# Input projection of a two-layer backbone with 512 moving columns instead of 256

## The chip, the cores and the metric

The kernel runs on one core of a Trainium2 chip, in one launch. The metric is the device time of that launch in microseconds. Five engines work side by side: TensorE (matmuls, PE in the profile, with its weight loads as PEld), VectorE (DVE), ScalarE (ACT), GpSimd (POOL) and SyncE (SP), which issues most DMAs.

## The reference, cut to what matters

Two layers run over 256 latent and 256 context tokens of width 1024, all fp32. Each layer normalises and modulates its input and projects it once, with a weight of 1024 x 2560, into ten column groups of 256:

```
h  = rms(x)   * (1 + sc_a)  + sh_a          # hc: the same for the context
aq, ak, av, hq, hff, hfb, hi, hg, gu, gv = split(h @ w_in[layer])
attn = window_attention(rope(rms(aq)), rope(rms(ak)), av, context keys, sink)
hg_l = rms(hgrn(silu(hq), hff, hfb, hi)) * gain * silu(hg)     # both directions
gm   = gelu(gu) * (w_s @ rms(gelu(gv)) + b_s)                  # chunks of 128
x    = x + g_a * (concat(attn, hg_l, gm) @ w_out[layer])
x    = x + g_f * channel_mixer(h')          # layer 0: SwiGLU, layer 1: top 2 of 8 experts
```

In layer 1 the context is needed only for the recurrence's states (hff, hfb, hi) and for keys and values (ak, av, together "akv"). The output is the latent stream.

## The kernel before, in words

An fp32 product is made of three matmuls of rounded operands, high x high, low x high and high x low (`mm3`, L241, which issues L244 to L246). The activations h are kept split in `hx`, one tile for each of the eight blocks k of 128 input channels. The weights stream from DRAM in tiles of 128 x 1024 (`Stream`): SP's queue loads a raw tile, ScalarE writes its high part (L125) and VectorE its low part (L126), half a tile at each `tick`. Two split pairs are held, four for a while in layer 1.

The projection is a generator (`proj`, L529). It goes through the ten column groups in the order `ORDER0` in layer 0, and `hff`, `hfb`, then `ORDER1` in layer 1 (L2032 to L2034); `akv` holds keys and values, `aq0` and `aq1` the two halves of the queries. A group (`group`, L553) works on tiles of 128 tokens, two of the context and two latent (`TTS`), or only the latent ones in layer 1 where the context isn't needed. Tokens are the loaded operand, weights the moving one, 256 columns wide. A weight tile holds four blocks k of one group, so a group has two halves kh; a step is one half for one tile of tokens, 12 matmuls, followed by one `tick` and a `yield`. Two tiles of tokens share a PSUM bank of 512 columns. After the second half of a tile of tokens, `evac_..` brings its columns out of PSUM: a copy on ScalarE for hi, akv and aq, Gelu for gu and gv in layer 1 (a copy in layer 0), and chains of Exp, Ln, Exp with VectorE between for hff, hfb, hq and hg.

There are eight banks, two named "mm", two "t" and four "u". The projection takes the least recently freed "mm" or "u" bank and leaves two "u" banks to others (`PSPARE`).

The mixer (`mixer`, L1195) advances the other work of the layer once for every yield of the projection: the recurrence `hg`, the gated mixing `gm`, key preparation and query statistics `at0`, and the attention proper `at1`. Each starts when the groups that it needs are complete (`HG_AT`, `GM_AT`, `AT0_AT`, `AT1_AT`), which is noticed when the projection yields the next group's name; a last group is never noticed there, and what waits for it starts when the projection is through. Then what is left runs, together with fillers (modulation chunks, the first half of the output projection, in layer 1 row transposes at L1377). The framework's scheduler takes the order of the program as priority and may put a ready instruction ahead of one that isn't, so emission order sets priorities, not the exact order on an engine.

After layer 1's mixer comes the expert stage: 352 MB of expert weights stream through a ring of tiles that the earlier stream leaves behind.

Of the kernel before, what the change touches and what calls it, by code (L numbers as in the profile page):

```python
# [21 lines left out]
P = 128  # L22
# [11 lines left out]
LAT = (0, 1)  # L34
CTX = (2, 3)
TTS = (2, 3, 0, 1)
# [36 lines left out]
class Stream:  # L73
# [3 lines left out]
    def __init__(self, nc, plan, mem, raw, hl):  # L77
        self.nc, self.plan, self.mem = nc, plan, mem
        self.n_dma = self.n_split = self.n_out = self.n_done = self.part = 0
        self.raw, self.hl = {}, {}  # L80
        self.raw_free, self.hl_free = deque(), deque()
        self.heir = None
        self.excess = 0
        self.grow(raw, hl)
# [112 lines left out]
class Gen:  # L197
# [326 lines left out]
        mem.put(y)  # L524


    ALL1 = ("hff", "hfb", "hi", "akv")

    def proj(self, l):  # L529

        if l == 0:
            for name in ORDER0:
                yield from self.group(l, name, TTS)
            return
        names = ("hff", "hfb")
        self.ws.grow(0, GROWP)
        ws = self.ws.need(4)
        for i, name in enumerate(names):
            yield from self.group(l, name, CTX, ws[2 * i:2 * i + 2])
        for i, name in enumerate(names):  # L540
            yield from self.group(l, name, LAT, ws[2 * i:2 * i + 2])
        self.ws.shrink(GROWP)
        for name in ORDER1:
            yield from self.group(l, name, TTS if name in ("hi", "akv") else LAT)

    @staticmethod
    def order(l):

        if l == 0:
            return ORDER0  # L550
        return ("hff", "hfb") + tuple(ORDER1)

    def group(self, l, name, tts, ws=None):  # L553

        tag = "ctx" if tts is CTX else name
        ps, bank, first = {}, {}, None
        if name not in self.st["open"]:
            self.st["open"].add(name)
            for _ in self.mem.room(4, 6 if name == "hff" else 2):
                yield tag  # L560
            self.opened(name, l)
        for tt in tts[::2]:
            while not any(len(self.banks[k]) > PSPARE[k] for k in ("mm", "u")):
                yield tag
            b = bank[tt + 1] = self.oldest("mm", "u", spare=PSPARE)
            ps[tt], ps[tt + 1] = b[:, :256], b[:, 256:]
        for kh in range(2):
            wh, wl = (x.rearrange("p (k n) -> p k n", k=4) for x in (ws[kh] if ws else self.ws.need()))
            for tt in tts:
                ts = slice(tt * P, tt * P + P)  # L570
                for k in range(4):
                    h = self.hx[4 * kh + k]
                    new = kh == 0 and k == 0
                    i = self.mm3(ps[tt], h[:, 0, ts], h[:, 1, ts], wh[:, k], wl[:, k], new and tt % 2 == 0,
                                 kh == 1 and k == 3)
                    if new:
                        if tt % 2:
                            self.after(i, first)
                        first = i
                if kh == 1:  # L580
                    while len(self.mem.free[1]) < 2:
                        yield tag
                    getattr(self, "evac_" + name[:2])(l, tt, ps[tt], name)
                    if tt in bank:
                        self.done(bank[tt])
                self.ws.tick()
                yield tag

# [224 lines left out]
    def hgrn_scores(self, tt):  # L813
# [17 lines left out]
        E[6] = yield from self.hgrn_expo(tt, 6)  # L831
        yield
        for n, lv in enumerate(order):
            if n < 3:
                E[order[n + 1]] = yield from self.hgrn_expo(tt, order[n + 1])
# [348 lines left out]
    def begin(self, l):  # L1184
# [8 lines left out]
        self.mx, self.mxt = {}, []  # L1193

    def mixer(self, l, proj, filler, masks=None):  # L1195

        mem = self.mem
        tts = TTS if l == 0 else LAT
        self.attn_tables(l)
        gm, hg = self.flagged("gm", self.gmlp(l, tts)), self.flagged("hg", self.hgrn(l))  # L1200
        unit = lambda tt, g: self.attn_tile(l, tt, g)
        if l == 0:
            at0 = self.chain(self.attn_keys(l), self.attn_qstats(tts, 0), self.weave(*[unit(tt, 0) for tt in tts], n=NAT))
            at1 = self.chain(self.attn_qstats(tts, 1), self.weave(*[unit(tt, 1) for tt in tts], n=NAT))
        else:
            at0 = self.chain(self.attn_keys(l), self.attn_qstats(tts, 0))
            at1 = self.chain(self.attn_qstats(tts, 1), self.weave(*[unit(tt, g) for tt in LAT for g in range(2)], n=NAT1))
        sides = []
        prev = None
        waits = [[set(n), g, r] for n, g, r in ((HG_AT[l], hg, R_HG[l]), (AT0_AT, at0, R_AT[l]), (GM_AT, gm, R_GM[l]),  # L1210
                                                (AT1_AT, at1, R_AT[l]))]
        seen = set()
        cs = None
        if l == 1:
            cs = self.flagged("cs", self.hgrn_ctx_states())
            waits.append([set(HG_AT[1]), cs, 2])

        def advance():
            for s, n in list(sides):
                for _ in range(n):  # L1220
                    if next(s, self) is self:
                        sides.remove((s, n))
                        break
        if masks:
            sides.append((masks, 1))
        for name in proj:
            if name != prev:
                seen.add(prev)
                for x in list(waits):
                    if x[0] <= seen and (x[1] is not at1 or waits[0][1] is at1 and at0 not in [z for z, _ in sides]):  # L1230
                        waits.remove(x)
                        sides.append((x[1], x[2]))
                if {"hff", "hfb"} <= seen and l == 1 and self.lbt is not None:
                    mem.put(self.lbt)
                    self.lbt = None
                prev = name
            advance()
        mem.put(*self.hx)
        self.run(cs, hg, gm, self.chain(at0, at1), filler)
        mem.put(self.st["kv"], *self.st["aq"], *self.st["KT"], self.rt)  # L1240
# [520 lines left out]
    def plan(self):  # L1761
        A = self.A
        f = lambda ap, w=1024: (ap.rearrange("p a b -> p (a b)"), w)
        w_in = lambda l: [f(A["w_in"][l, COLS.index(n), h]) for n in self.order(l) for h in range(2)]
        plan = w_in(0) + [f(A["w_out0"][h, d]) for h in range(2) for d in range(4)]
        for half in range(2):
            plan += [f(A["ffn_gu"][11 * half + j, z]) for j in range(11) for z in range(2)]
            for d in list(range(8)) * (1 + half):
                plan += [f(A["ffn_d"][half, d][:, f0:f1, :], (f1 - f0) * P) for f0, f1 in ((0, 6), (6, 11))]
        plan += w_in(1) + [f(A["w_out1"][dh, 2 * a + b]) for a in range(2) for dh in range(2) for b in range(2)]  # L1770
        return plan
# [69 lines left out]
    def build(self):  # L1841
        nc, tc, A = self.nc, self.tc, self.A
        with ExitStack() as ctx:
# [7 lines left out]
            ps = ctx.enter_context(tc.tile_pool(name="ps", bufs=1, space=PSUM))  # L1851
# [15 lines left out]
            w = [self.ada_load(0, n) for n in (0, 2)]  # L1867
# [13 lines left out]
            next(nm)  # L1881
            for _ in range(4):
                next(nm)
            for _ in range(4):
                next(proj)
            self.run(self.ada_chunk(0, 1, w[2]))
            self.run(self.ada_chunk(0, 3, w[3]))
            self.run(nm)
            mem.put(*self.Xt)
            masks = self.load_masks()  # L1890
            for _ in range(4):
                next(proj)

            def filler0():
# [129 lines left out]
PSPARE = dict(mm=0, u=2)  # L2024
# [4 lines left out]
NAT = 4  # L2029
NAT1 = 4  # L2030
GROW0A = 2
COLS = ("hff", "hfb", "hi", "hq", "akv", "aq0", "aq1", "hg", "gu", "gv")  # L2032
ORDER0 = ('hi', 'hq', 'hff', 'hfb', 'aq0', 'aq1', 'hg', 'gu', 'gv', 'akv')
ORDER1 = ('gu', 'gv', 'akv', 'aq0', 'aq1', 'hi', 'hq', 'hg')  # L2034
EARLY = (0, 1)
HG_AT, R_HG = (('hff', 'hfb'), ('hff', 'hfb', 'gv', 'hi', 'hq')), (1, 2)
GM_AT, R_GM = ("gu", "gv"), (1, 1)
# [36 lines left out]
def _layout(inp):  # L2074
    g = {k: np.asarray(v) for k, v in inp.items()}
    c = np.ascontiguousarray
    d = _consts()
# [7 lines left out]
    d["bcol"] = c(g["b_ada"].reshape(2, 48, P).transpose(2, 0, 1))  # L2085
    o = dict(aq0=(0, 256), aq1=(256, 512), akv=(512, 768), hq=(768, 1024), hff=(1024, 1280), hfb=(1280, 1536),
             hi=(1536, 1792), hg=(1792, 2048), gu=(2048, 2304), gv=(2304, 2560))
    cols = np.concatenate([np.arange(*o[n]) for n in COLS])
    w = g["w_in"][:, :, cols]
    d["w_in"] = c(w.reshape(2, 2, 4, P, 10, 256).transpose(0, 4, 1, 3, 2, 5))  # L2090
    w = g["w_out"]
    d["w_out0"] = c(w[0].reshape(KD, P, KD, P)[list(Gen.KORD)].reshape(2, 4, P, 4, 2, P).transpose(0, 3, 2, 4, 1, 5)
                    .reshape(2, 4, P, 8, P))
# [1 line left out]
    gu = np.stack([g["ffn_w_gate"][0], g["ffn_w_up"][0]], 0)  # L2095
# [27 lines left out]
```

## Time and profile before

| | us |
|---|---|
| median of three runs | 1830.62 (1826.94 to 1834.07) |
| the profiled execution | 1828.56 |
| its span | 1826.8 |
| projection of layer 0, first and last matmul | about 25 to 183 |
| projection of layer 1 | 717 to 820 |
| expert stage | from about 930 |

The granted TensorE clock is 1.00 in both projections, and 0.987 over the span. A line of the profile's groups names the output before the arrow and the operands behind it, moving operand first; "mm" and "u" are PSUM banks. Matmuls overlap, so the time that one costs in a stream is the distance of two starts.

### The profile page before, as it was taken

The page shows a single profiled execution, that of the slowest core. Times are in us where ns is not written, and L with a number is a line of the kernel's source. Part 1 is how long each engine was busy: PE and PEld are TensorE (multiplying, and loading weights), DVE is VectorE, ACT ScalarE, POOL GpSimd, SP SyncE. Part 2 cuts the span into 40 slices and gives each one's busy share as a digit, 9 for nine tenths or more (in the row PEclk, how much of TensorE's full clock was granted, in tenths as well). Part 3 has the DMA queues.
Part 4 walks back from the last instruction along what each step waited for, and adds up shares of the span by engine and source line. Part 5 has one row for each costly group of instructions (what it writes and reads, how often), then busy time and mean ns, then how long its engine had stood idle before and what let it go on. Part 6 is the DMA issues. An engine that isn't in the chain of part 4 may idle for free. (4 is left out here: it accounts for less than half of the span.)

```text
span 1826.8 us, 34724 instructions
## 1 busy us (share of the span) xinstructions
PE 1744.1 (95%) x14056; PEld 1077.7 (59%) x14057; DVE 774.9 (42%) x1924; ACT 536.0 (29%) x1203; POOL 33.3 (2%) x56
## 2 busy tenths in 40 slices
PE   6999999999999999999989998999989999999997
PEld 3999778988788898998843333333333333333333
DVE  4556986899664378868720011110212011120112
ACT  4654656623222356765410010100101010010100
POOL 1000000100000001000000000000000000000000
PEclk9999999999999999999989999999999999999998
DMA  9224342367763255330589999999999999999990
GB/s 347 75 84 138 136 150 70 127 243 234 233 234 123 85 158 173 96 116 13 211 326 381 401 408 407 406 406 401 397 405 406 403 403 400 402 408 402 403 391 31
DMA packets 137006, 485.64 MB, mean 266 GB/s; under 512 B 15888, under 2 KB 17040, under 8 KB 136784
## 3 DMA queue, kind: packets, MB, share of 16 engines
q1 hardware_dynamic: 136080, 480.08, 69.3%
q8 instruction: 168, 2.75, 0.6%
q0 software_dynamic: 704, 2.36, 0.4%
q14 instruction: 54, 0.44, 0.1%
HBM read 481.33 MB, written 1.05 MB: 264 GB/s over the span
## 5 line engine op out<-in xcount | busy, mean ns | idle before, releaser
L1580 PE MATMUL u<-wr,xg 128*32 128x512 f32 (+1 forms) x5376 | 525.6, 546 | 18.5 <-issue 13.4
L1580 PEld LDWEIGHTS u<-wr,xg 128*32 128x32 f32 x5376 | 174.0, 111 | 342.6 <-issue 291.5
L1580 PE MATMUL mm<-wr,mT 128*32 128x512 f32 x2352 | 260.8, 593 | 4.3 <-ACT mh L264 1.5
L125 ACT ACTIVATE hi<-raw 128x512 fp32r<-128x512 f32 (+2 forms) x296 | 160.6, 580 | 244.5 <-PE u L246 90.6
L126 DVE TENSOR_TENSOR lo<-raw,hi 128x512 fp32r<-128x512 f32 (+2 forms) x296 | 178.7, 634 | 106.6 <-ACT hi L125 105.4
L1613 DVE TENSOR_TENSOR mh<-mh,u 128x512 f32<-128x512 f32 (+1 forms) x32 | 19.8, 619 | 411.1 <-PE u L1580 256.9
L1580 PEld LDWEIGHTS mm<-wr,mT 128*32 128x32 f32 x2352 | 77.6, 110 | 175.7 <-issue 152.0
L264 ACT ACTIVATE mh<-u 128x512 f32<-128x512 f32 (+1 forms) x64 | 34.6, 540 | 414.2 <-PE u L1580 413.7
L244 PE MATMUL u<-hx,hi 128*128 128x512 f32 (+1 forms) x384 | 142.9, 372 | 0.8 <-DVE X L1288 0.8
L245 PE MATMUL u<-hx,lo 128*128 128x512 f32 (+1 forms) x384 | 142.6, 371 | 0.0
L246 PE MATMUL u<-hx,hi 128*128 128x512 f32 (+1 forms) x384 | 142.6, 371 | 0.0
L264 ACT ACTIVATE mT<-t 128x512 f32<-128x512 f32 (+1 forms) x32 | 17.4, 544 | 256.4 <-PE t L1625 255.5
L245 PE MATMUL mm<-fx,lo 128*128 128x256 f32 (+1 forms) x264 | 85.0, 322 | 5.6 <-DVE lo L126 5.5
L244 PE MATMUL mm<-hi,hx 128*128 128x256 f32 x288 | 84.9, 296 | 3.8 <-ACT hx L264 3.0
L1631 DVE COPY mT<-t 128x256 f32<-128x256 f32 (+1 forms) x32 | 12.5, 391 | 170.8 <-PE t L1630 170.8
L244 PE MATMUL mm<-fx,hi 128*128 128x256 f32 (+1 forms) x264 | 84.4, 320 | 0.6 <-ACT hi L125 0.6
L246 PE MATMUL mm<-fx,hi 128*128 128x256 f32 (+1 forms) x264 | 83.9, 318 | 0.0
L245 PE MATMUL mm<-hi,hx 128*128 128x256 f32 x288 | 82.2, 287 | 0.4 <-DVE hx L521 0.3
L246 PE MATMUL mm<-lo,hx 128*128 128x256 f32 x288 | 81.7, 285 | 0.0
L244 PEld LDWEIGHTS u<-hx,hi 128*128 128x128 f32 x384 | 72.3, 188 | 13.6 <-DVE X L1288 1.0
L245 PEld LDWEIGHTS u<-hx,lo 128*128 128x128 f32 x384 | 72.3, 188 | 12.6
L246 PEld LDWEIGHTS u<-hx,hi 128*128 128x128 f32 x384 | 72.3, 188 | 12.3
(344 smaller groups left out, 2600.4 us busy)
## 6 DMA issues: line engine op xcount, KB each, us to landing
wr<-in_moe_g SPq DMA_DIRECT2D x224, 512.0 KB, 10.1
wr<-in_moe_u SPq DMA_DIRECT2D x224, 512.0 KB, 10.1
wr<-in_moe_d SPq DMA_DIRECT2D x224, 512.0 KB, 10.1
adat<-in_w_adaT SPq DMA_DIRECT2D x56, 512.0 KB, 4.8
raw<-in_ffn_gu SPq DMA_DIRECT2D x44, 512.0 KB, 3.5
adaw<-in_w_ada SPq DMA_DIRECT2D x40, 512.0 KB, 6.3
raw<-in_w_in SPq DMA_DIRECT2D x40, 512.0 KB, 3.6
raw<-in_ffn_d SPq DMA_DIRECT2D x24, 384.0 KB, 3.6
```

Source lines behind the costliest of these rows:

```text
L125: nc.scalar.activation(h[:, s], r[:, s], AF.Copy)
L126: nc.vector.tensor_tensor(l[:, s], r[:, s], h[:, s].bitcast(F32), op=ALU.subtract)
L244: i = mm(ps, lh, rh, start=start, stop=False, skip_group_check=True)
L245: mm(ps, ll, rh, start=False, stop=False, skip_group_check=True)
L246: self.final = mm(ps, lh, rl, start=False, stop=stop, skip_group_check=True)
L264: i = self.nc.scalar.activation(out, in_, func, **kw)
L1580: self.nc.tensor.matmul(bank[c:c + 32, :n], lhsT, rhs, start=start, stop=stop, tile_position=(0, c), skip_group_check=True)
L1613: nc.vector.tensor_tensor(h[:, 0, :n], h[:, 0, :n], U[:, :n], op=ALU.mult)
L1631: nc.vector.tensor_copy(hT[:, :m, :, 64:], pt[:, :m * 64].rearrange("p (j a s) -> p j a s", j=m, a=2))
```

## The change

Column groups go in pairs, five in each layer (`PAIRS`), with 512 moving columns: one matmul covers both groups. A tile of tokens has a whole bank, so a pair holds four banks (two in layer 1 where only latent or only context tokens run). A weight tile holds two blocks k of a pair, so a pair is worked in four parts; a step is two blocks for one tile of tokens, 6 matmuls. The bank of a tile of tokens is taken at its step of the first part and given back after its step of the last, where both groups are evacuated one after the other. The name that the mixer sees is that of the pair, and both names count as complete when the next pair begins. In layer 0 eight steps instead of four are emitted at each of the two places ahead of the mixer.

```diff
+    def group(self, l, names, tts, ws=None):
+        tag = "ctx" if tts is CTX else "+".join(names)
+        bank = {}
...
+        for i in range(4):
+            wh, wl = (x.rearrange("p (k n) -> p k n", k=2) for x in (ws[i] if ws else self.ws.need()))
             for tt in tts:
                 ts = slice(tt * P, tt * P + P)
...
+                if i == 0:
+                    while not any(len(self.banks[k]) > PSPARE[k] for k in ("mm", "u")):
                         yield tag
+                    bank[tt] = self.oldest("mm", "u", spare=PSPARE)
+                for k in range(2):
+                    h = self.hx[2 * i + k]
+                    self.mm3(bank[tt], h[:, 0, ts], h[:, 1, ts], wh[:, k], wl[:, k], i == 0 and k == 0,
+                             i == 3 and k == 1)
+                if i == 3:
+                    for z, name in enumerate(names):
+                        while len(self.mem.free[1]) < 2:
+                            yield tag
+                        getattr(self, "evac_" + name[:2])(l, tt, bank[tt][:, 256 * z:256 * z + 256], name)
+                    self.done(bank[tt])
                 self.ws.tick()
                 yield tag
...
-                seen.add(prev)
+                seen.update((prev or "").split("+"))
...
-            for _ in range(4):
+            for _ in range(8):
                 next(proj)
...
-ORDER0 = ('hi', 'hq', 'hff', 'hfb', 'aq0', 'aq1', 'hg', 'gu', 'gv', 'akv')
-ORDER1 = ('gu', 'gv', 'akv', 'aq0', 'aq1', 'hi', 'hq', 'hg')
+PAIRS = ((("hi", "hq"), ("hff", "hfb"), ("aq0", "aq1"), ("hg", "gu"), ("gv", "akv")),
+         (("hff", "hfb"), ("gu", "gv"), ("akv", "hi"), ("aq0", "aq1"), ("hq", "hg")))
```

## Rows read from the trace of the kernel before

**Rows 1.** The page, part 1: engines' busy us, share of the span, instructions.

```profile
PE 1744.1 (95%) x14056; PEld 1077.7 (59%) x14057; DVE 774.9 (42%) x1924; ACT 536.0 (29%) x1203; POOL 33.3 (2%) x56
```

**Rows 2.** Windows by stage; the first line names the columns.

```profile
core 0: us, PE busy (x) PEld busy (x) DVE busy (x) ACT busy (x) POOL busy (x), PEclk, DMA share, GB/s
...
90.00:188.00 98.00, 97.03 (x839) 92.08 (x838) 60.91 (x201) 50.45 (x110) 2.41 (x6) 1.00 0.36 123
188.00:260.00 72.00, 68.88 (x548) 52.88 (x546) 63.38 (x262) 42.45 (x123) 0.56 (x2) 1.00 0.40 142
...
750.00:820.00 70.00, 69.40 (x569) 67.38 (x569) 49.08 (x151) 46.13 (x115) 1.23 (x4) 1.00 0.39 129
820.00:890.00 70.00, 69.29 (x542) 61.95 (x540) 60.47 (x202) 37.89 (x88) 0.56 (x2) 1.00 0.15 52
```

**Rows 3.** Waits of PE, 20 to 260: us in total, times, longest.

```profile
PE mm L244 <- ACT hx L264: 3.0, 3, 2.7
PE mm L1084 <- ACT pp L264: 1.7, 1, 1.7
```

**Rows 4.** Windows in the expert stage, columns as in rows 2.

```profile
930.00:940.00 10.00, 10.00 (x96) 3.20 (x95) 0.08 (x1) 0.81 (x1) 0.00 (x0) 1.00 0.31 107
...
1000.00:1100.00 100.00, 96.06 (x944) 36.48 (x940) 12.07 (x19) 11.30 (x24) 0.00 (x0) 1.00 1.02 404
```

**Rows 5.** Windows of PE's work on `hx`, the projections: busy (count), clock, DMA.

```profile
20.00:188.00 168.00, 128.54 (x960) 0.98 0.41 145
715.00:825.00 110.00, 86.85 (x672) 1.00 0.35 116
```

**Rows 6.** Timeline of PE in layer 1's projection: start, us, engine, line, operation.

```profile
761.77 0.28 PE L244 MATMUL u<-hi,hx 128*128 128x256 f32 x1
...
764.53 0.28 PE L246 MATMUL u<-lo,hx 128*128 128x256 f32 x1
```

**Rows 7.** Timeline of PE in the feed-forward layer.

```profile
399.75 0.39 PE L245 MATMUL u<-hx,lo 128*128 128x512 f32 x1
...
411.99 0.39 PE L245 MATMUL u<-hx,lo 128*128 128x512 f32 x1
```

**Rows 8.** Timeline of PE in layer 1's output projection, tokens loaded, weights moving.

```profile
907.47 0.39 PE L246 MATMUL u<-lo,mx 128*128 128x512 f32 x1
...
910.01 0.39 PE L245 MATMUL u<-hi,mx 128*128 128x512 f32 x1
```

**Rows 9.** Timeline of ACT: one evacuation of hff, then two half splits.

```profile
71.67 0.38 ACT L264 ACTIVATE ge<-u 128x256 f32<-128x256 f32 x1 [0.41 <-PE u L246]
72.42 0.51 ACT L264 ACTIVATE gg<-ge,ones 128x256 f32<-128x256 f32 x1 [0.36 <-DVE ge L645]
72.96 0.42 ACT L264 ACTIVATE hk<-gg 128x256 f32<-128x256 f32 x1
73.28 0.40 ACT L264 ACTIVATE hg<-gg 128x256 fp32r<-128x256 f32 x1
...
82.19 1.15 ACT L125 ACTIVATE hi<-raw 128x512 fp32r<-128x512 f32 x2 [2.61 <-PE mm L245]
```

**Rows 10.** Windows of DVE's work on `uv`, then on `gsq`, layer 0.

```profile
150.00:188.00 38.00, 4.64 (x12) 1.00 0.54 183
...
150.00:188.00 38.00, 1.57 (x4) 1.00 0.54 183
```

**Rows 11.** Windows of DVE's work on `kk`, `kdup`, `aq`, `qt`, in that order.

```profile
765.00:820.00 55.00, 6.62 (x30) 1.00 0.35 116
...
765.00:820.00 55.00, 1.90 (x8) 1.00 0.35 116
...
765.00:820.00 55.00, 9.13 (x32) 1.00 0.35 116
...
765.00:820.00 55.00, 1.67 (x4) 1.00 0.35 116
```

**Rows 12.** Timeline of PE: layer 1's first and last projection matmul, row transposes, first scores.

```profile
717.00 0.37 PE L244 MATMUL u<-hi,hx 128*128 128x256 f32 x1
...
819.73 0.28 PE L246 MATMUL mm<-lo,hx 128*128 128x256 f32 x1
...
828.55 1.95 PE L1377 MATMUL t<-ident,mods 128*128 128x128 f32 x16
...
830.25 0.47 PE L1084 MATMUL mm<-KT,qt 128*128 128x512 f32 x1
```

More of the change, by code (lines that the diff above doesn't have):

```diff
@@ L524, in norm_mod @@
         mem.put(y)
-    ALL1 = ("hff", "hfb", "hi", "akv")
     def proj(self, l):
         if l == 0:
-            for name in ORDER0:
-                yield from self.group(l, name, TTS)
+            for names in PAIRS[0]:
+                yield from self.group(l, names, TTS)
             return
-        names = ("hff", "hfb")
         self.ws.grow(0, GROWP)
         ws = self.ws.need(4)
[L538 to L541, printed above, removed]
+        for tts in (CTX, LAT):
+            yield from self.group(l, PAIRS[1][0], tts, ws)
@@ L542, in proj @@
         self.ws.shrink(GROWP)
[L543 to L568, printed above, removed]
+        for names in PAIRS[1][1:]:
+            yield from self.group(l, names, TTS if "hi" in names else LAT)
@@ new lines, in group @@
+    def group(self, l, names, tts, ws=None):
+        tag = "ctx" if tts is CTX else "+".join(names)
+        bank = {}
+        for name in names:
+            if name not in self.st["open"]:
+                self.st["open"].add(name)
+                for _ in self.mem.room(4, 6 if name == "hff" else 2):
+                    yield tag
+                self.opened(name, l)
+        for i in range(4):
+            wh, wl = (x.rearrange("p (k n) -> p k n", k=2) for x in (ws[i] if ws else self.ws.need()))
@@ L569, in group @@
             for tt in tts:
                 ts = slice(tt * P, tt * P + P)
[L571 to L579, printed above, removed]
@@ L580, in group @@
-                if kh == 1:
-                    while len(self.mem.free[1]) < 2:
-                        yield tag
-                    getattr(self, "evac_" + name[:2])(l, tt, ps[tt], name)
-                    if tt in bank:
-                        self.done(bank[tt])
+                if i == 0:
+                    while not any(len(self.banks[k]) > PSPARE[k] for k in ("mm", "u")):
+                        yield tag
+                    bank[tt] = self.oldest("mm", "u", spare=PSPARE)
[3 more added lines that the diff above has]
+                             i == 3 and k == 1)
@@ L586, in group @@
+                if i == 3:
+                    for z, name in enumerate(names):
+                        while len(self.mem.free[1]) < 2:
+                            yield tag
+                        getattr(self, "evac_" + name[:2])(l, tt, bank[tt][:, 256 * z:256 * z + 256], name)
+                    self.done(bank[tt])
                 self.ws.tick()
@@ L1763, in plan @@
         f = lambda ap, w=1024: (ap.rearrange("p a b -> p (a b)"), w)
-        w_in = lambda l: [f(A["w_in"][l, COLS.index(n), h]) for n in self.order(l) for h in range(2)]
+        w_in = lambda l: [f(A["w_in"][l, n, h]) for n in range(5) for h in range(4)]
         plan = w_in(0) + [f(A["w_out0"][h, d]) for h in range(2) for d in range(4)]
@@ L1890, in build @@
             masks = self.load_masks()
-            for _ in range(4):
+            for _ in range(8):
                 next(proj)
@@ L2031 @@
 GROW0A = 2
-COLS = ("hff", "hfb", "hi", "hq", "akv", "aq0", "aq1", "hg", "gu", "gv")
-ORDER0 = ('hi', 'hq', 'hff', 'hfb', 'aq0', 'aq1', 'hg', 'gu', 'gv', 'akv')
-ORDER1 = ('gu', 'gv', 'akv', 'aq0', 'aq1', 'hi', 'hq', 'hg')
+PAIRS = ((("hi", "hq"), ("hff", "hfb"), ("aq0", "aq1"), ("hg", "gu"), ("gv", "akv")),
+         (("hff", "hfb"), ("gu", "gv"), ("akv", "hi"), ("aq0", "aq1"), ("hq", "hg")))
 EARLY = (0, 1)
@@ L2087, in _layout @@
              hi=(1536, 1792), hg=(1792, 2048), gu=(2048, 2304), gv=(2304, 2560))
-    cols = np.concatenate([np.arange(*o[n]) for n in COLS])
-    w = g["w_in"][:, :, cols]
-    d["w_in"] = c(w.reshape(2, 2, 4, P, 10, 256).transpose(0, 4, 1, 3, 2, 5))
+    cols = [np.concatenate([np.arange(*o[n]) for ns in PAIRS[l] for n in ns]) for l in range(2)]
+    d["w_in"] = c(np.stack([g["w_in"][l][:, cols[l]].reshape(4, 2, P, 5, 512).transpose(3, 0, 2, 1, 4)
+                            for l in range(2)]))
     w = g["w_out"]
```

## The prediction

> **What bounds the kernel now.** I read the page's busy shares first: TensorE is busy 95% of the span [rows 1], so a change pays if it takes time from TensorE or from a chain that TensorE waits for. The windows by stage come next. While layer 0 projects (90 to 188) TensorE is busy 97.0 of 98 us, in layer 1 (750 to 820) 69.4 of 70 [rows 2]. There VectorE is the second engine, at 60.9 of 98 and 49.1 of 70. Right behind each projection it is nearly full as well: 63.4 of 72 us (188 to 260) and 60.5 of 70 us (820 to 890), which leaves 8.6 and 9.5 us free [rows 2]. The list of waits of TensorE from 20 to 260 is short: 3.0 us for the normed input and under 2 us for anything else [rows 3]. So the projection is a matter of TensorE's cadence, and the stretch behind it one of TensorE and VectorE together. The expert stage is the rest: from 1000 to 1100 the DMA queues are saturated at 404 GB/s and TensorE is 96% busy, but at 930 to 940 DMA rests at a share of 0.31, since the ring of weight tiles is full and TensorE has only begun [rows 4]. The expert stage therefore starts when the layers before it end, and moves earlier or later as a whole; what the projection wins reaches the end.
>
> **The change part by part.**
>
> *Half as many matmuls, each twice as wide.* The projection has 960 matmuls of 256 columns in layer 0 and 672 in layer 1 [rows 5]. Afterwards there are 480 and 336 of 512 columns, 816 in all, and as many weight loads. The price is the time from start to start, not the duration of a row, for matmuls overlap. 256 columns: 24 in a row start from 761.77 to 764.53, 2.76 / 23 = 0.120 us [rows 6]. 512 columns in the feed-forward layer: 399.75 to 411.99 in 54 steps, 0.2267 us [rows 7]. 512 columns with tokens as the loaded operand and weights moving, which is the form that the change brings: 907.47 to 910.01 in 11 steps, 0.231 us [rows 8]. One wide matmul for two narrow ones saves 0.0133 us by the one row, 0.009 by the other: 10.9 or 7.3 us for 816. I take 7.3 us, the same form (4.3 in layer 0, 3.0 in layer 1), and keep 10.9 as the upper end.
>
> [...]
>
> *Order and pace.* A step was 12 narrow matmuls, now 6 wide ones; a weight tile still serves four steps (two in the split stage of layer 1), is still 512 KB, and there are still 40, so SP's queue and the splitting of weights on ScalarE and VectorE keep their pace: no cost. The first part of layer 0 is emitted as 8 steps ahead of the second pair of modulation chunks where it was 4: the same inputs, the same columns that can run before the later half of the normed input arrives. The 3.0 us wait for that input [rows 3] can only shrink; I count nothing, at most 0.7 us.
>
> *Evacuations in bursts.* Both halves of a pair are evacuated in the last four of sixteen steps. The worst pair is hff with hfb: one evacuation has four activations, 0.38 + 0.51 + 0.42 + 0.40 = 1.71 us [rows 9], so a step brings 3.4 us, plus 0.6 us for half a weight tile (1.15 for two), about 4.0 us of ScalarE against 6 x 0.231 = 1.39 us of TensorE. Four steps make 16 us, which TensorE outruns by 10.7 us. What waits is the next pair, where it needs a bank of this one. It takes the least recently used banks: two are free, and their tiles' first two parts give 4 steps, 5.5 us of cover; so between 0 and 5.2 us are lost there, once. Afterwards the evacuated pairs are light (copies), and the split stage of layer 1 has two tiles instead of four. I take 0: TensorE has recurrence work ready besides.
>
> *Four banks held instead of two.* The projection now keeps four of eight banks, and the recurrence, which asks for two "u" banks at once, has two left. It may get on more slowly beside layer 0's projection.
>
> *Gated mixing in layer 0 starts later.* It waits for gu and gv; gv was ahead of akv, now both are in the last pair, so nothing of it is emitted until the projection ends, 8 steps later. Of its VectorE work 4.6 us on uv and 1.6 us on the squares ran before 188 [rows 10], 6.2 us that now fall into a stretch with 8.6 us free. Its two small DMAs on POOL's queue move with it. With the slower recurrence I price this between 0 and 6.2 us and take 1.5, near the low end because 6.2 fits into 8.6.
>
> *Attention in layer 1 starts later.* akv was evacuated by step 32 of 56, now by step 40, aq0 and aq1 by 36 and 40, now 48; key preparation was released at step 36, now at 48 (hi comes 8 steps sooner, which helps the context states). A step there takes (820 - 717) / 56 = 1.8 us [rows 12]. VectorE spent 6.6 + 1.9 us on keys and 9.1 + 1.7 us on queries from 765 to 820, all beside the projection [rows 11]: 19.3 us. Now the keys (8.5 us) have the last 8 steps, some 14 us, and the queries fall behind the end, into 9.5 us of room. Bounds: 0 if all is absorbed, 19.3 - 9.5 = 9.8 us if none of it runs before the projection's end. I take 1.5. In layer 1 Gelu of gu and gv now comes in one burst, still with one table load each way: nothing.
>
> Sum: -7.3 + 0 + 1.5 + 1.5 = -4.3 us. The profiled execution took 1828.56 us (span 1826.8, 1.8 around it), so 1824.3 us for the same execution; it lies 2.1 us under the median of the three runs, 1830.62, and from that median it is **1826.3 us**.
>
> **Rivals.**
>
> *A, the whole gain.* The wide cadence is the feed-forward one, 10.9 us, the startup wait loses its 0.7, and VectorE absorbs everything: 1830.6 - 11.6 = 1819.0. For it: TensorE is full, so work that is put off just fills it later, and after 820 it has transposes that depend on neither (L1377) [rows 12]. Against: rows 8, not 7, are the same form.
>
> *B, attention of layer 1 becomes late (the other side).* VectorE's 19.3 us of keys and queries lie behind the projection, and the first score matmul, at 830.25 now, 10.5 us after the last projection matmul (819.73) [rows 12], slips. It decides once the moved work exceeds the 9.5 us of VectorE's room after 820; priced at 9.8: -7.3 + 9.8 + 1.5 = +4.0, 1834.6, with layer 0's 6.2 us in full 1839.3. For it: VectorE is 86% busy there. Against: TensorE waits for nothing long in that stretch now.
>
> *C, the bank wait.* TensorE stalls 5.2 us behind the burst of hff and hfb: -4.3 + 5.2 = +0.9, 1831.5. For it: ScalarE's 16 us in four steps. Against: the covers named.
>
> *D, no cadence to win.* Beside evacuations the wide matmul has already lost 4 ns of its 13 (0.2267 to 0.231); if it loses 6.5 more in the projection, 2.5 ns are left, 2.0 us: -2.0 + 3.0 = +1.0, 1831.6. [...] Against: 0.231 was measured while ScalarE and VectorE worked.
>
> **How the numbers follow.** Forecast 0.34, A 0.24, B 0.22, C 0.13, D 0.07. A measurement of this kernel can tell about 0.5% (9.2 us) from no change. Faster than 1821.5: most of A and a part of the forecast's spread, 0.30. Slower than 1839.8: the tail of B, and B with C, 0.14. Within: 0.56. The range takes in A with some of its spread and B with layer 0's price: 1814 to 1840; the forecast's own range is 1821 to 1832.
>
> **What would show it.** 816 projection matmuls, starting 0.23 us apart; the last of layer 0 some 4 us earlier or more, since less is woven in. Waits of TensorE for the evacuations of hff or hfb would show C. A longer stretch from the last projection matmul of layer 1 to the first score matmul, with VectorE above 90%, would show B. A cadence of 0.237 would show D. The prediction is wrong in kind if the stretch behind either projection grows by more than 7 us, or if the expert stage, from its first wide matmul to the end, changes its length by more than 3 us.

## The result, and the profile after

The changed kernel takes 1862.54 us (median of 4 runs, 1856.02 to 1865.85), the kernel before beside it 1830.97: a ratio of 1.0168 with a 95% interval of 1.0148 to 1.0188. It is 31.6 us slower. The forecast was 1826.3 with a range of 1814 to 1840, so it was wrong in sign and the range missed. The profiled execution has 1860.28 us, its span 1858.5.

The first part of the page [rows 1] shows the 816 matmuls less. TensorE is busy 2.5 us longer all the same, so the time isn't in added work.

```profile
PE 1746.6 (94%) x13240; PEld 1042.1 (56%) x13241; DVE 774.0 (42%) x1924; ACT 530.5 (29%) x1203; POOL 34.0 (2%) x56
```

The windows of the projections and of the expert stage in the kernel after (columns as in [rows 2]) answer to [rows 2, 4]:

```profile
90.00:172.00 82.00, 81.94 (x478) 67.10 (x476) 49.59 (x160) 38.99 (x87) 2.51 (x6) 1.00 0.40 135
...
200.00:210.00 10.00, 6.89 (x44) 5.81 (x44) 9.16 (x43) 5.38 (x13) 0.00 (x0) 0.76 0.06 25
...
750.00:800.00 50.00, 49.88 (x240) 41.23 (x240) 38.18 (x126) 31.52 (x79) 0.95 (x3) 1.00 0.46 158
```

```profile
930.00:940.00 10.00, 10.00 (x96) 3.18 (x92) 0.00 (x0) 0.28 (x1) 0.00 (x0) 1.00 0.34 111
1000.00:1100.00 100.00, 91.80 (x882) 35.39 (x878) 12.07 (x19) 11.31 (x24) 0.00 (x0) 0.98 0.98 381
```

The projections are as full as before, and layer 0 is through sooner: the feed-forward layer begins at 335.7 us instead of 339.9. The stage that the change doesn't touch is the one that differs. From 1000 to 1100 TensorE is busy 91.8 us where it was 96.1, and the transfers come at 381 GB/s where they came at 404 [rows 4]. The first matmul on an expert's weights starts at 929.3 us (before: 929.9). From there to the last one the stage takes 911.0 us where it took 879.7. That is 31.3 of the 31.7 us by which the two spans differ.

TensorE's groups in this stage, before and after (out<-in, shapes, count, busy us, mean ns, idle us before them and what ended it), say what kind of time it is. Before:

```profile
L1580 PE MATMUL u<-wr,xg 128*32 128x512 f32 x4032 | 443.0, 594 | 5.4 <-issue 4.2 <-DMA wr<-in_moe_g 1.2
L1580 PE MATMUL mm<-wr,mT 128*32 128x512 f32 x2352 | 260.8, 593 | 4.3 <-ACT mh L264 1.5 <-DMA wr<-in_moe_g 1.0 <-issue 0.8
L1580 PE MATMUL u<-wr,xg 128*32 128x256 f32 x1344 | 82.6, 400 | 13.0 <-issue 9.2 <-DMA wr<-in_moe_g 3.8
```

After:

```profile
L1563 PE MATMUL u<-wr,xg 128*32 128x512 f32 x4032 | 449.5, 598 | 14.5 <-issue 14.5
L1563 PE MATMUL mm<-wr,mT 128*32 128x512 f32 x2352 | 266.7, 608 | 21.4 <-issue 13.5 <-DMA wr<-in_moe_d 7.7 <-ACT mT L264 0.2
L1563 PE MATMUL u<-wr,xg 128*32 128x256 f32 x1344 | 78.3, 380 | 9.8 <-issue 9.8
```

The same matmuls; but "issue", time in which TensorE waits for no semaphore that the profile sees, has grown from 4.2 and 0.8 us to 14.5 and 13.5 in the wide groups. In the narrow one it was there before the change too: 9.2 us, and 9.8 after. SP's queue shows the other end, first before, then after (who waited for whom, us in total, times, longest):

```profile
SPq L179 <- DMA wr<-in_moe_d: 169.5, 190, 2.6
...
SPq L179 <- PE u L1580: 75.2, 71, 8.2
```

```profile
SPq L179 <- PE u L1563: 282.0, 123, 8.9
SPq L179 <- DMA wr<-in_moe_d: 96.7, 114, 1.8
```

Before, SP mostly waits for earlier transfers, so the transfers set the pace. After, it mostly waits for TensorE to give a buffer of the ring back, and meanwhile the transfers rest (381 GB/s above instead of 404).

**What TensorE waits for.** Its timeline in the kernel after, around two such waits (start, us, engine, line, operation, count, idle before):

```profile
1025.62 2.31 PE L1563 MATMUL u<-wr,xg 128*32 128x256 f32 x34
1029.89 10.51 PE L1563 MATMUL mm<-wr,mT 128*32 128x512 f32 x96 [1.96 <-DMA wr<-in_moe_d]
...
1044.21 4.48 PE L1563 MATMUL u<-wr,xg 128*32 128x512 f32 x24 [3.17 <-issue]
```

The first is put down to a transfer. But the tile that this matmul reads, the 73rd of the ring, had landed at 998.1 us, 32 us earlier: a transfer that happened to land then got the name. The DMA queues over two short windows, 1026.9 to 1027.3 and 1041.5 to 1042.1, show what both waits have in common:

```profile
q8 instruction: 1, 0.02, 16.1%
```

```profile
q8 instruction: 1, 0.02, 9.7%
```

In each a packet of the instruction queue q8 starts, at 1027.07 and at 1041.81. The waits end 2.8 and 2.4 us later. I take these packets for TensorE's own code from their number: from 34 to 929 us before the change, TensorE shows 5828 matmuls and 5826 weight loads, and the queue 46 packets of together 0.75 MB, so 253 instructions in 16.3 KB; after it 5021, 5019 and 40 packets, so 251. Before:

```profile
34.00:929.00 895.00, 872.98 (x5828) 767.92 (x5826) 638.12 (x1703) 436.96 (x1019) 27.19 (x42) 0.99 0.44 149
```

```profile
q8 instruction: 46, 0.75, 0.3%
```

In the expert stage there are 120 packets before and 119 after, one each 7.3 and 7.7 us. Each part of an expert's work has two branches, one with and one without the third block of tokens, and the code of the branch that isn't taken is jumped over, though its packets still come: 120 packets at 256 (an estimate from the 253) hold some 30,700 instructions, and TensorE executes 16,300 matmuls and weight loads there. I took all idle times of TensorE over 0.5 us in the stage: but for 4, which stand before transposes and wait for VectorE (6.5 us together in either kernel), each ended 2.3 to 2.9 us after the start of such a packet. Before there are 17, 21.1 us together, after 24, 45.1 us. After the second of the two waits above the granted clock falls, and the next rows are slower too, groups of four matmuls 0.86 us apart instead of 0.43:

```profile
1040.00:1044.00 4.00, 1.04 (x8) 0.40 (x4) 0.29 (x1) 0.38 (x1) 0.00 (x0) 1.00 0.98 381
1044.00:1048.00 4.00, 3.79 (x24) 1.12 (x28) 0.00 (x0) 0.00 (x0) 0.00 (x0) 0.61 0.81 328
```

TensorE is busy 1.04 of 4 us, then the granted clock is 0.50 from 1044.9 to 1048.3, and the transfers come at 328 GB/s there instead of 381.

The theory, CODE: the change takes 1632 matmuls and weight loads out of the code ahead of the stage and adds 12 semaphore instructions. That is 1620, and with blocks of 256 instructions, the same estimate, six of them and 84 more. So every branch of the expert stage lies 84 places earlier in the blocks in which its code is fetched, and there TensorE runs into blocks that are still on their way more often. Two rivals fit the trace as well: SLOTS (the ring has 30 buffers in both kernels, but 12 of its places hold another one) and ARRIVAL (its first 15 tiles are asked for in another order).

### The profile page after: what moved, and what is told of

The parts are those of the page before. It is cut to its first block, busy times and chain, and to the rows that moved or that the text cites. A ratio compares the mean times of both kernels' runs of the same rounds, so it can differ in the third digit from the quotient of the medians.

```text
span 1858.5 us, 33113 instructions
## 1 busy us (share of the span) xinstructions
PE 1746.6 (94%) x13240; PEld 1042.1 (56%) x13241; DVE 774.0 (42%) x1924; ACT 530.5 (29%) x1203; POOL 34.0 (2%) x56
## 3 DMA queue, kind: packets, MB, share of 16 engines
HBM read 481.33 MB, written 1.05 MB: 260 GB/s over the span
## 5 line engine op out<-in xcount | busy, mean ns | idle before, releaser
L1563 PE MATMUL mm<-wr,mT 128*32 128x512 f32 x2352 | 266.7, 608 | 21.4 <-issue 13.5
L264 ACT ACTIVATE mh<-u 128x512 f32<-128x512 f32 (+1 forms) x64 | 34.6, 541 | 414.8 <-PE u L1563 414.3
L245 PE MATMUL mm<-fx,lo 128*128 128x256 f32 (+1 forms) x264 | 85.7, 325 | 5.4 <-DVE lo L126 5.2
L447 DVE SCALAR_TENSOR_TENSOR adat<-adat,silb 128x1024 f32<-128x1024 f32 x56 | 68.2, 1222 | 14.2 <-DMA adat<-in_w_adaT 13.5
L1672 DVE SCALAR_TENSOR_TENSOR xt<-t,gate,xt 128x512 f32<-128x512 f32 x32 | 22.6, 746 | 122.5 <-PE t L1670 122.4
L244 PE MATMUL u<-hi,hx 128*128 128x512 f32 x160 | 64.2, 404 | 4.3 <-ACT hx L264 4.3
```

The source lines that it names most:

```text
L244: i = mm(ps, lh, rh, start=start, stop=False, skip_group_check=True)
L245: mm(ps, ll, rh, start=False, stop=False, skip_group_check=True)
L264: i = self.nc.scalar.activation(out, in_, func, **kw)
L447: nc.vector.scalar_tensor_tensor(w[i] if z == zs - 1 else junk, w[i], 1.0, sil[z], op0=ALU.mult, op1=ALU.mult, accum_out=self.mods[l][:, c ...
L1563: self.nc.tensor.matmul(bank[c:c + 32, :n], lhsT, rhs, start=start, stop=stop, tile_position=(0, c), skip_group_check=True)
L1672: nc.vector.scalar_tensor_tensor(self.xt[tt][:, s], ps, gate[:, tt], self.xt[tt][:, s], op0=ALU.mult, op1=ALU.add)
```

## The experiments

**Shift the code and nothing else.** Small matmuls of zeros at the start, where TensorE waits for data (before the change up to 12.3 us), move all code behind them. Each is four instructions, two loads and two matmuls, as the trace of the kernel before has 160 loads and 160 matmuls for the 80 fp32 matmuls of L395. The order of all other instructions on all engines stays as it was; only one semaphore instruction of TensorE ahead of the stage falls away, so the places below are exact to one.

```diff
             self.act(self.sil[:, :, 0:2], cT, AF.Silu)
+            for _ in range(43):        # 21, 64, 10, 37, 53 in the others
+                nc.tensor.matmul(self.banks["t"][0][:32, :32], self.zero, self.zero, start=True, stop=True,
+                                 skip_group_check=True)
```

> The kernel before, with 43 small fp32 matmuls of zeros (172 instructions of TensorE, no use made of them) at the very start, where TensorE waits for data anyway. They move the code of the expert stage by 172 places within the blocks of 256 instructions (16 KB) in which TensorE's code is fetched; the change moved it by 84 the other way (1620 instructions fewer ahead of it), which is the same place. Theory CODE (the place of the code in the fetch blocks sets how often TensorE waits for its instructions): the expert stage, 880 us before, takes 905 to 915 us, the whole 1855 to 1867. Rival SLOTS (the buffers that the ring of weight tiles got are others after the change) and rival ARRIVAL (the first tiles of the ring were asked for in another order): nothing changes here, 878 to 883 us, the whole 1827 to 1836.

Measured: 1870.74 us, ratio to before 1.0212 (1.0191 to 1.0233). The stage takes 916.7 us. The old projection with its code shifted has the loss of the new one. The whole is 3.7 us above what was expected: the layers ahead of the stage took 8.3 us more in the profiled execution, in small pieces at a low clock (0.98 to 0.99 up to layer 1, where the kernel before has 0.99 to 1.00), and why isn't settled.

> The kernel after, with 21 such matmuls (84 instructions) at the very start: its expert stage then lies in the fetch blocks as it does before the change. CODE: the expert stage takes 877 to 883 us instead of 911, the whole 1825 to 1833. SLOTS and ARRIVAL: the stage stays at 908 to 914 us and the whole at 1858 to 1866.

Measured: 1829.57 us, ratio 0.9995 (0.9977 to 1.0012), stage 877.1 us. The changed kernel with 84 idle instructions in front loses nothing. Its buffers and its order of first tiles are those of the change, so SLOTS and ARRIVAL fall. The groups show where the time went back:

```profile
L1563 PE MATMUL u<-wr,xg 128*32 128x512 f32 x4032 | 442.4, 594 | 5.2 <-issue 4.5 <-DMA wr<-in_moe_d 0.6
L1563 PE MATMUL mm<-wr,mT 128*32 128x512 f32 x2352 | 261.0, 593 | 3.6 <-DMA wr<-in_moe_g 1.5 <-ACT mh L264 1.5 <-issue 0.4
```

> The kernel before with 64 of the small matmuls (256 instructions, one whole fetch block) at the very start. CODE says that only the place within a block counts: the expert stage is back at 877 to 883 us and the whole at 1827 to 1838. Rival COUNT (any added instructions, or the work at the start, cost the time of the shift by 172): 40 us or more on the whole, 1865 to 1880.

Measured: 1835.40 us, ratio 1.0014 (0.9998 to 1.0029), stage 880.3 us. More instructions than in the first experiment, and no loss: it is the place in the block that counts, and a shift by 256 leaves it where it was (879.7 without). COUNT falls.

> The kernel after with 10 small matmuls (40 instructions) at the very start: a place between that of the change (0, stage 911.0 us) and that of the kernel before (84, stage 877.1 us). CODE: the stage is a function of the place in the block of 256 with 911 at 0, 877 at 84, and no more than the transfers' 869 and some 920 as its ends; here something between, 877 to 911. SLOTS: refuted already; COUNT would have it at 911 plus what the matmuls cost, under 2 us.

> The same with 37 small matmuls (148 instructions), past the place of the kernel before. CODE gives 869 to 920 us for the stage and no better figure: it shows whether 84 is the best place or lies on a slope. Each wait of TensorE of 2 us or more for no semaphore should again end 2.4 to 2.9 us after the start of a 16 KB instruction packet.

> The same with 53 small matmuls (212 instructions), the last quarter ahead of 256, where the place is that of the change again (911 us): 869 to 920 us, and nearer to 911 than the place 148 if the stage changes steadily with the place.

Measured: 1857.70 (1.0121, 1.0057 to 1.0185), 1836.59 (1.0023, 1.0003 to 1.0042) and 1851.31 (1.0104, 1.0067 to 1.0142). The shift by 212 is nearer to the change than that by 148, as a steady slope would have it. At place 148 the three idle times of over 2 us ended 2.5 to 2.6 us after the start of a packet, as expected. By place (that of the change is 0), with the idle times over 0.5 us that ended 2.2 to 2.9 us after a packet's start, without those before transposes, which wait for VectorE (one more, of 1.2 us at place 40, ended 2.97 us after):

| kernel, place | stage, us | such idle times | together, us |
|---|---|---|---|
| after, 0 | 911.0 | 24 | 45.1 |
| after, 40 | 904.0 | 24 | 42.0 |
| after, 84 | 877.1 | 12 | 19.0 |
| after, 148 | 886.5 | 19 | 25.5 |
| after, 212 | 902.2 | 19 | 34.6 |
| before, 84 | 879.7 | 17 | 21.1 |
| before + 256, 84 | 880.3 | 15 | 20.4 |
| before + 172, 0 | 916.7 | 24 | 45.8 |

The kernel before stood at the best of the places tried, and the change moved it to the worst. Why one place has more such waits than another was not worked out. The whole times follow the stage only roughly, for it doesn't start at the same time in all of them: at 936.4 us after the shift by 256 and at 936.2 after that by 40, 6.5 and 6.8 us later than without, but 1 to 2 us earlier after those by 84, 148 and 212. That isn't settled either.

**Less code to fetch.** The matmuls that both branches share leave the branches.

```diff
-            for arm in self.arms(e):
...
-                        self.four(G, n, ((b0, ga), (b1, ga), (b0, gb), (b1, gb)), *z)
-                        self.four(U, n, ((b0, ua), (b1, ua), (b0, ub), (b1, ub)), *z)
-                        if arm:
-                            self.four(X, n, ((b2, ga), (b2, gb), (b2, ua), (b2, ub)), *z)
+            for z, (b0, b1, b2), (ga, gb, ua, ub) in steps:
+                self.four(G, n, ((b0, ga), (b1, ga), (b0, gb), (b1, gb)), *z)
+                self.four(U, n, ((b0, ua), (b1, ua), (b0, ub), (b1, ub)), *z)
+            with self.tc.If(self.third[e] > 0):
+                for z, (b0, b1, b2), (ga, gb, ua, ub) in steps:
+                    self.four(X, n, ((b2, ga), (b2, gb), (b2, ua), (b2, ub)), *z)
```

The down projection (`moe_down`) is changed in the same way.

> The kernel after, with the matmuls that both branches of an expert share taken out of the branches, so that only the third block of tokens is conditional: about 2400 instructions for an expert in place of 3850, the same matmuls executed (the third block's behind the others of its half). CODE: the stage fetches about 75 blocks instead of 122 and TensorE waits for hardly any; it comes down to what the transfers need, 865 to 882 us, the whole 1813 to 1832. SLOTS and ARRIVAL: 905 us or more, the whole 1855 to 1866, since rings and slots are as after the change.

> The same edit on the kernel before. CODE: the stage takes 865 to 880 us, within 4 us of the same edit on the kernel after, the whole 1815 to 1831; what is left between the two is the projection itself. SLOTS and ARRIVAL: 878 to 883 us, some 30 us less than the same edit on the kernel after.

> The kernel after with the shared matmuls out of the branches, and 32 small matmuls (128 instructions) at the very start, half a fetch block. CODE: with 75 blocks in the stage instead of 122 there is time to fetch at any place, so the stage stays within 6 us of the 868.7 us it takes without the shift, the whole at 1815 to 1825. If the 868.7 us were a lucky place: 880 us or more.

Measured: 1818.83 (0.9935, 0.9911 to 0.9959), 1818.53 (0.9936, 0.9915 to 0.9958) and 1818.49 us (0.9937, 0.9914 to 0.9959); the stage 868.7, 868.9 and 869.1 us. The changed kernel's stage from 931 to 1801 has 74 packets, its 100 us as in [rows 4] are full, and no "issue" is left in the groups:

```profile
q8 instruction: 74, 1.21, 0.6%
```

```profile
1000.00:1100.00 100.00, 98.37 (x972) 37.01 (x968) 12.32 (x20) 11.41 (x24) 0.00 (x0) 1.00 1.03 408
```

```profile
L1563 PE MATMUL u<-wr,xg 128*32 128x512 f32 x4032 | 450.7, 593 | 3.6 <-DMA wr<-in_moe_u 2.8 <-PEq L1592 0.5
L1563 PE MATMUL mm<-wr,mT 128*32 128x512 f32 x2352 | 263.5, 593 | 3.6 <-DMA wr<-in_moe_d 2.8 <-PEq L1592 0.5 <-ACT mT L264 0.2
```

One idle time that ends 2.2 to 2.5 us behind a packet's start is left in each of the three, of 1.2, 1.1 and 0.6 us. Half a block of shift changes nothing any more. And with the code out of the way, the old projection and the new one come out equal: 1818.53 and 1818.83. So the change itself is worth nothing that these runs can tell.

**Where the projection's own gain goes.** With the old projection layer 1 takes 212.1 us from its first projection matmul to the expert stage, with the new one 215.8 (windows of the two kernels with the shared code, old first):

```profile
716.92:929.00 212.08, 203.27 (x1542) 188.31 (x1541) 162.32 (x503) 126.08 (x310) 6.01 (x11) 0.98 0.39 134
```

```profile
715.76:931.60 215.84, 203.91 (x1206) 174.96 (x1204) 161.12 (x503) 123.63 (x310) 6.05 (x11) 0.96 0.40 134
```

TensorE is idle 3 us more, and has a lower clock. Two experiments change only the order of the pairs in layer 1, on the kernel with the shared code:

```diff
-         (("hff", "hfb"), ("gu", "gv"), ("akv", "hi"), ("aq0", "aq1"), ("hq", "hg")))
+         (("hff", "hfb"), ("gu", "gv"), ("akv", "hi"), ("hq", "hg"), ("aq0", "aq1")))    # hg first
+         (("hff", "hfb"), ("gu", "gv"), ("akv", "hi"), ("hq", "aq0"), ("aq1", "hg")))    # mixed
```

> The kernel after with the shared matmuls out of the branches, and in layer 1 the pair of hq and hg ahead of that of aq0 and aq1. With the change layer 1 takes 215.8 us from the first projection matmul to the expert stage where the old projection takes 212.0. Theory RECURRENCE (in layer 1 the recurrence waits for hq, which stands in the last pair, so it starts only when the projection is through, and its chain ends last): it starts a pair sooner, the 2.5 us wait of TensorE for its state and the slow clock behind it go, and the stretch takes 210 to 213 us, the whole 1813 to 1817. Rival ATTENTION (the prediction's rival B: keys and queries are late): these come a pair later still, and the stretch takes 218 us or more, the whole 1820 or more.

> The same, with the last two pairs of layer 1 mixed: hq with aq0, then aq1 with hg. Recurrence, keys and the first half of the queries are all complete when the last pair begins; only aq1 is late. RECURRENCE: 209 to 213 us for the stretch, as with hq and hg ahead. ATTENTION: 213 to 216 us. Both: the whole at 1812 to 1819, not above the kernel without this edit (1818.8).

Measured: 1823.65 us (0.9958, 0.9941 to 0.9975) and 1811.80 us (0.9894, 0.9877 to 0.9911). The windows, hg first and then mixed:

```profile
712.78:935.50 222.72, 205.94 (x1205) 174.64 (x1203) 162.39 (x504) 124.56 (x310) 6.01 (x11) 0.93 0.40 131
```

```profile
715.98:924.90 208.92, 199.22 (x1205) 169.56 (x1202) 161.24 (x503) 123.73 (x310) 6.03 (x11) 0.98 0.43 139
```

RECURRENCE alone is refuted: with hq and hg ahead the whole is some 5 us slower than with the changed order (1823.65 to 1818.83), where a gain was expected. The stretch grows by 7 us, as ATTENTION said, and the first row of TensorE's waits there (780 to 930) is for queries:

```profile
PE t L1049 <- DVE qt L1043: 2.6, 2, 2.4
```

How long the stretch is varies by several us: in the changed order it took 214.4 to 222.2 us in seven kernels, the 222.2 at a clock of 0.94, the 215.8 above at 0.96. So the whole times weigh more here than one window. ATTENTION alone doesn't give the mixed order's result either, 208.9 us and a whole 7.0 us faster, in which the recurrence and the keys are both released when the last pair begins and the keys come no earlier; it had 213 to 216. What fits all three orders: whichever of the two is released only after the projection sets the end. In the changed order it is the recurrence, and TensorE's longest wait from 780 to 925 is for its state; in the mixed order that wait is gone (the first rows of the waits, after the change and mixed):

```profile
PE u L1815 <- DVE ST L852: 2.5, 1, 2.5
PE t L1815 <- DVE oh L1521: 1.9, 1, 1.9
```

```profile
PE t L1817 <- DVE oh L1521: 1.9, 1, 1.9
PE t L1454 <- DVE xt L1403: 1.4, 1, 1.4
```

The mixed order with the shared code beats both kernels, by 1.06% and by 2.7%.

## Why the prediction was wrong

**The step that failed** is in its first part: "The expert stage therefore starts when the layers before it end, and moves earlier or later as a whole; what the projection wins reaches the end." It started 0.6 us earlier, and did not move as a whole: it grew by 31 us. I took the stage for one that the transfers pace and whose work is the same, so its length could not change. But TensorE has only 4 us in 100 to spare there [rows 4], its code is fetched in 16 KB blocks, and how those lie depends on every instruction ahead: moved by 172, the old stage took 916.7 us instead of 879.7. None of the rivals had this. The prediction did name the sign that would show it wrong in kind, a stage that changes by more than 3 us. The loss has nothing to do with the sizes of the sum's terms. That the kernel before stood at the best of the places tried was chance.

Not only jumps are hit: of the changed kernel's 24 waits of 45.1 us, the one of 1.7 us that ends at 1111 us stands some 20 matmuls into a branch of 32.

**The cadence** was sized too small. The wide matmuls start 0.227 us apart in layer 1 (median, as in the feed-forward layer [rows 7], rival A's figure, and not the 0.231 of [rows 8]), the narrow ones 0.120 [rows 6]. With the shared code, all projection matmuls together take 126.2 + 86.3 us to the start of the next instruction in the old form, 117.4 + 80.0 in the new: 15.1 us less, where 7.3 were taken and 10.9 was the upper end. What exceeds the cadence's 10.9 lies in the distances to other work between them; that it is the smaller number of switches was only argued. D is refuted: no run shows the 2.5 ns a matmul that its 2.0 us is made of, and by the measured distances a wide one saves 2 x 0.120 - 0.227 = 0.013 us.

**Layer 0** gained more than the -4.3 + 1.5 of the sum. From the first projection matmul to the feed-forward layer the four kernels with the old projection take 314.9 to 318.5 us (mean 316.6), nine with the new one 309.1 to 312.5 (310.7): -5.8. The projection itself got 10.1 us shorter from its first to its last matmul (156.4 to 146.3), since less is woven in, and the stretch behind it 6.1 us longer. The window from 200 to 210 above has the price of the late work: 6.9 us busy of 10, and a clock of 0.76, where the kernel before has 10.0 and 1.00.

**Layer 1** was the wrong sign: -3.0 + 1.5 taken, +3.5 measured (212.0 to 214.4 us in four kernels, mean 212.8; 214.4 to 222.2 in seven, mean 216.4). The projection got 17.0 us shorter (102.7 to 85.7), but the stretch from its last matmul to the expert stage 20.1 us longer (110.1 to 130.2). That is the prediction's other sign of being wrong in kind, 7 us behind a projection. Rival B had the place and the kind, work that is released too late, though it priced the layer at -3.0 + 9.8 = +6.8. Its own sign came by half: the first score matmul follows the last projection matmul after 18.0 us instead of 10.5, but VectorE is busy 75% of them, not above 90%. It blamed keys and queries; in the changed order the work that ended last was the recurrence, whose start in layer 1 waits for hq (`HG_AT`), and hq had moved into the last pair, which is never noticed. I read that rule for attention and didn't read it for the recurrence.

**The bank wait** (C) did not come: TensorE's longest waits from 20 to 260 us are for the normed input, 4.3 us in all, and for the modulation, 2.8. Taking the burst of evacuations at nothing was right. That first wait grew from 3.0 [rows 3] and did not shrink. C's own sum is a little off: four steps at 4.0 us against 1.39 leave 10.4 us and not 10.7, so 4.9 behind the cover of 5.5.

Without the expert stage the two layers come to -5.8 + 3.5 = -2.3 us for -4.3 predicted. That this is near is luck in part: layer 0 came out 3.0 us better than its terms and layer 1 5.0 us worse. The kernel after with its code shifted back takes 1829.57, 3.3 us above the forecast and inside its own range, but the 2.8 us that it is ahead of the kernel before beside it (1832.35) are not clear of the noise (ratio up to 1.0012), and with the shared code the change gives nothing (1818.83 to 1818.53).

## What to carry to other kernels

A change that adds or removes instructions moves all code behind it. Where a later stage has branches and little slack, time it with a shift of the code before the change is judged: 84 idle instructions gave back 1.8% here and 172 took 2.1%, where the edit itself is worth less than 0.3%. "issue" time, and waits put down to a transfer that had long landed, were the sign (14.5 and 13.5 us in the wide groups, and a tile that had landed 32 us earlier); compare them with the starts of the instruction packets. Keep what two branches share outside of them (868.7 us for the stage here instead of 911.0). And when groups are merged, look up for each consumer which is its last group, and whether that one's end is noticed.

## What the runs showed of the hardware

A 16 KB packet of code took about 1.05 us (mean in the changed kernel's stage, nearly all 0.88 to 1.11), yet the waits in the table were over only 2.2 to 2.9 us after a packet's start.

Some of these waits were followed by a lower granted clock and others not: in the changed kernel's stage the 4 us behind those of 3.17, 3.51, 3.64 and 3.73 us and behind one of 2.00 us have a granted clock of 0.50 to 0.65, those behind one of 3.10 us and another of 2.00 us 1.00. So the wait of 3.17 us cost more than itself: behind it the groups of four matmuls start 0.86 us apart instead of 0.43.

The stage grows with these waits, but not one for one. From 869 us with one wait of 1.2 us it gains 8 to 12 us where they come to 19 to 21 us, 18 us at 25.5, and 42 to 48 us at 45 to 46.
